# Transposing DMAs of the softmax weights beside the attention of a hybrid decoder trunk

## The chip, the core and the metric

The kernel runs on one core of a Trainium2 chip. The metric is the device time of one execution in microseconds. A core has TensorE (matmuls, in the profile PE, with its weight loads as PEld), VectorE (DVE), ScalarE (ACT), GpSimd (POOL) and SyncE (SP). SyncE computes nothing here; it issues nearly all DMAs, in the order of its queue, and a DMA that has to wait for something holds back every DMA behind it. A "q" behind an engine's name in the profile (SPq) means its sequencer.

## The reference

Two residual layers over one sequence of 1,024 positions and width 1,024, then a final RMS norm. The first layer is a gated linear recurrence (RG-LRU), the second forgetting attention with 16 heads of width 64, which is where the change lies:

```python
def one_block(args):
    q_blk, cq_blk, start = args
    qpos = start + jnp.arange(Q_BLOCK, dtype=jnp.int32)
    logits = jnp.einsum("bqhd,bkhd->bhqk", q_blk.astype(jnp.float32), kf) * scale
    logits = logits + (cq_blk[..., :, None] - ck[:, :, None, :])
    mask = kpos[None, :] <= qpos[:, None]
    logits = jnp.where(mask[None, None], logits, NEG_INF)
    p = jax.nn.softmax(logits, axis=-1)
    return jnp.einsum("bhqk,bkhd->bqhd", p, vf)
...
o = lax.map(one_block, (qb, cqb, starts))
...
y = o * jax.nn.silu(gate)
return y @ w_out.astype(h.dtype)
```

Queries go in blocks of 128 (`Q_BLOCK`). Block i, from 0 to 7, sees keys 0 to 128(i+1) - 1. `p`, the softmax weights of a block, is what the change touches.

## The kernel before, in words

All matmuls are done in split float32: each operand is divided into a high part (rounded to fp32r) and a low remainder, and three products are summed (`to_hi`, L85 and L87, mostly on ScalarE; `to_lo`, L96, on VectorE or GpSimd).

The first layer fills about the first 450 us. Attention follows, head by head. The work of a head is written as Python generators:

- `kq_units` and `g_units` project keys, queries and gates of the next pair of heads (products `gps`). `weights` loads each of their weight tiles `wf` (SyncE, L109) into one of three buffers and splits it into `wh` and `wl`. `values`, once in four heads, projects the values of the next two pairs (`vps`); in that stretch nothing else of a head runs.
- `load` and `load_q` (L604 to L618) copy a head's keys into tile T and its queries into tiles U, through SyncE. The tiles hold one head (T, two in turn) or half a head (U), so a copy waits until the matmuls of the head before have read the tile. The U of the first four blocks is one tile that all heads share.
- `maxima(hd, c)` takes blocks 4c to 4c + 3 of head hd. For each block it makes the logits S by matmuls of U and T (L54), adds the mask and finds the row maximum on VectorE (L715), and takes the exponential on ScalarE (L720), which writes `p` with its row sums. The tile of block i has one buffer for all heads, so block i of the next head overwrites it, about 29 us later. The exponential's instruction is kept in `seen`.
- `weigh(hd, c)` transposes p on TensorE by the identity (`pt`, L58), splits the result into `ph` and `pl` (three buffers each) and multiplies by the values (`O`). `scale` and `gated` multiply by the gate; `yo` is stored to DRAM by SyncE (L808).
- At the end `turned(c, q)` adds the output projection to the residual, transposed into rows (`turn`), takes squares for the norm (`sq1`, L931, ScalarE, in a tile `xp` with two buffers) and multiplies by the norm's weight.

`run` sets the order on TensorE: a hand-written string such as `1.0.1.1.1.0.0` says in which order the next step of `weigh` (0), of `maxima` for the coming half head (1) and of the filling projections (a dot) are taken. The order of the instructions on each engine, the DMAs in SyncE's queue among them, is fixed when the program is built; a planner may place instructions that no string orders, such as DMAs, by its own estimate.

Of the kernel before, what the change touches and what calls it, by code (L numbers as in the profile page):

```python
# [11 lines left out]
F32 = mybir.dt.float32  # L12
# [5 lines left out]
P = 128  # L18
SEQ = 1024
HALF = 512  # L20
# [18 lines left out]
def trunk(ctx: ExitStack, tc: tile.TileContext, xt, w0, wg, wo0, pc, gn, gf, w1, wv, wf, bf, wo1, out):  # L39
    nc = tc.nc  # L40

    def pool(name, bufs, **kw):
        return tc.tile_pool(name=name, bufs=bufs, **kw)
# [9 lines left out]
    def matmul(*args, **kw):  # L53
        pe[0] = nc.tensor.matmul(*args, **kw)  # L54
        return pe[0]
# [127 lines left out]
    with ExitStack() as l0:  # L183
# [9 lines left out]
        def long(tag, dtype=F32, bufs=1):  # L193
            return tmp.tile([P, SEQ], dtype, tag=tag, name=tag, bufs=bufs)
# [56 lines left out]
        sq = [z[:, cs] for z in (long("th"), long("ti")) for cs in halves]  # L251
# [240 lines left out]
    with ExitStack() as l1:  # L492
        tu = l1.enter_context(pool("tu", 1))
        at = l1.enter_context(pool("at", 2))
# [197 lines left out]
        def maxima(hd, c):  # L692

            s = hd % 2
            pair = hd // 2
            if c == 0:
                stats[hd] = at.tile([P, 8], F32, tag="sums", name="sums")
            sums = stats[hd]
            for i in range(4 * c, 4 * c + 4):
                n = (i + 1) * P  # L700

                o_ = 192 if i == 4 else 0
                S = ps.tile([P, SEQ], F32, tag="S", name="S")[:, o_:]
                u = U[s][c]
                qs = slice(i % 4 * P, i % 4 * P + P)
                for lo_, hi_ in ((0, min(n, HALF - o_)), (HALF - o_, n)):
                    if hi_ <= lo_:
                        continue
                    hi_ = max(hi_, lo_ + 256)
                    matmul(S[:, lo_:hi_], u[:, 0, qs], T[s][:, 0, lo_:hi_], start=True, stop=False)  # L710
                    matmul(
                        S[:, lo_:hi_], u[:96, 1, qs], T[s][:96, 1, lo_:hi_], start=False, stop=True
                    )
                m = at.tile([P, 1], F32, tag="m", name="m", bufs=4)
                nc.vector.tensor_tensor_reduce(  # L715
                    S[:, :n], S[:, :n], mask[:, SEQ - n :], -1.0, -NEG, ALU.add, ALU.min, accum_out=m
                )

                p = ps_[i] = at.tile([P, n], F32, tag=f"p{i}", name="p", bufs=1)
                seen[0] = nc.scalar.activation(  # L720
                    p, S[:, :n], AF.Exp, bias=m, scale=-1.0, accum_out=sums[:, i : i + 1]
                )
                yield
            if hd == HEADS - 1 or c == 1:
                b0, b1 = (4 * c if hd == HEADS - 1 else 0), 4 * c + 4
                nb = b1 - b0
                sums = sums[:, b0:b1]
                nc.vector.tensor_scalar(sums, sums, 2.0, None, ALU.mult)
                nc.vector.reciprocal(sums, sums)
                tr = ps.tile([P, P], F32, tag="O", name="tr")  # L730
                nc.tensor.transpose(tr[:nb], sums, ident)
                rc = at.tile([8, P], F32, tag="rc", name="rc", bufs=1)
                nc.vector.tensor_copy(rc[:nb], tr[:nb])
                nc.gpsimd.dma_start(recd[hd, b0:b1], rc[:nb])
                if s == 0:
                    recs[pair] = at.tile([P, SEQ], F32, tag="recb", name="recb", bufs=1)
                rows = slice(s * HD, (s + 1) * HD)
                nc.gpsimd.dma_start(
                    recs[pair][rows, b0 * P : b1 * P],
                    recd[hd : hd + 1, b0:b1].rearrange("o b q -> o (b q)").to_broadcast([HD, nb * P]),  # L740
                )
                yield
# [142 lines left out]
        def residual(c, q):  # L885

            cs = slice(q * 256, (q + 1) * 256)
            if c == q == 0:
                xs = [vpool.tile([P, 256], F32, tag=f"v{d}", name="x1", bufs=2) for d in range(KT)]
                for d, x in enumerate(xs):  # L890
                    nc.sync.dma_start(x, x1d[c, :, d, cs])
                return xs
            xs = [wpool.tile([P, 2, 256], F32, tag=("wl", "wh")[q], name="x1") for d in range(4)]
            for d, x in enumerate(xs):
                nc.sync.dma_start(x, x1d[c, :, 2 * d : 2 * d + 2, cs])
            return [x[:, i] for x in xs for i in range(2)]

        def turned(c, q):


            xs = left.pop((c, q), None) or residual(c, q)

            if c == 0:
                res = tu.tile([P, 2, SEQ], F32, tag=f"T{q}", name="res")
                res = [res[:, b] for b in range(2)]
            elif q == 0:
                res = [tu.tile([P, SEQ], F32, tag=t, name="res") for t in ("U", "U0")]
            else:
                res = [tu.tile([P, SEQ], F32, tag="U1", name="res"), at.tile([P, SEQ], F32, tag="p7", name="res", bufs=1)]
            for b in range(2):  # L910
                cs = slice(q * 256 + b * P, q * 256 + (b + 1) * P)

                parts = ((0, 4), (4, 2), (6, 2)) if c * q * b else ((0, 4), (4, 4))
                ss = ssq[c][:, 4 * q + 2 * b :][:, : len(parts)]
                for h, (d0, nd) in enumerate(parts):
                    hs = slice(d0 * P, (d0 + nd) * P)
                    pt = ps.tile([P, HALF], F32, tag="gO"[c * b] if h < 2 else "g", name="turn")[:, : nd * P]

                    for i in range(nd):
                        x = xs[d0 + i][:, b * P : (b + 1) * P]  # L920
                        matmul(pt[:, i * P : (i + 1) * P], x, ident, start=i == 0, stop=False, is_transpose=True)
                    for k in range(2):
                        yh, yl = (z[:, cs] for z in y1[c][6 + k])
                        wh, wl = (z[:, k::2][:, d0 % 4 : d0 % 4 + nd] for z in late_w[d0 // 4])
                        matmul(pt, yh, wh, start=False, stop=False)
                        matmul(pt, yl, wh, start=False, stop=False)
                        matmul(pt, yh, wl, start=False, stop=k == 1)
                        if k == 0:
                            yield
                    sq = at.tile([P, HALF], F32, tag="xp", name="sq1", bufs=2)[:, : nd * P]  # L930
                    nc.scalar.activation(sq, pt, AF.Square, accum_out=ss[:, min(h, ss.shape[1] - 1)].unsqueeze(1))  # L931
                    if c == 0 or h < len(parts) - 1:
                        nc.vector.tensor_tensor(res[b][:, hs], pt, grow[:, hs], ALU.mult)
                        if h == 1 and c == 1:
                            nc.vector.tensor_tensor(ss[:, 0:1], ss[:, 0:1], ss[:, 1:2], ALU.add)
                            ss = ss[:, 0::2]
                        yield
                if c == 1:
                    r = root_mean(ss, lambda: nc.vector.tensor_tensor(res[b][:, hs], pt, grow[:, hs], ALU.mult))
                    lo, hi = halves  # L940
                    nc.scalar.activation(res[b][:, lo], res[b][:, lo], AF.Copy, scale=r)
                    nc.vector.tensor_scalar(res[b][:, hi], res[b][:, hi], r, None, ALU.mult)
                    for hs in halves:
                        nc.sync.dma_start(out[4 + 2 * q + b, :, hs], res[b][:, hs])
                    yield
            if c == 0:
                first_half.extend(res)

        def root_mean(ss, between=lambda: None):

            ss = ss.rearrange("p (b h) -> p b h", h=2)
            r = ss[:, :, 0]
            nc.vector.tensor_tensor(r, r, ss[:, :, 1], ALU.add)
            between()
            nc.scalar.activation(r, r, AF.Sqrt, bias=epst, scale=1.0 / SEQ)
            nc.vector.reciprocal(r, r)
            return r
# [28 lines left out]
        load(0, halves[1], (1,))  # L986
        load(1, halves[1], (1,))
        run("00.0.0", maxima(0, 0), fill=fill)
        load_q(1, 0)
        drain(fill)  # L990
        for hd in range(HEADS):
# [31 lines left out]
            if hd % 4 == 3 and hd < 12:  # L1023

                vals = values(hd // 4 + 1)
                next(vals)
            run(second, weigh(hd, 1), maxima(hd + 1, 0), fill=fill, side=side)
            drain(side)
            gated(hd, 1)
# [93 lines left out]
```

## Time and profile before

| | |
|---|---|
| three runs | 1123.03, 1123.92, 1126.91 us; median 1123.92 |
| span of the profiled execution, the only time the page gives for it | 1127.7 us |
| instructions in the trace | 15,774 |
| TensorE, VectorE, ScalarE, GpSimd busy | 99%, 67%, 52%, 17% |
| DMA bytes | 105.43 MB, mean 93 GB/s |

The page gives, for each engine, the time in which it was busy, and then the chain that ended last: the work that, followed back from the last instruction, set the end. Issuing a DMA is not counted as busy time, so SyncE's load does not show among the busy shares; its queue shows in the list of DMA issues, in its waits and in the timeline. The views by windows give busy time in chosen stretches of the span, the views by tile or line the instructions that belong to it and what ended their waits.

### The profile page before, as it was taken

The numbers are of one execution on the slowest core, as the hardware profiler recorded it, in microseconds if no ns is written. First come the engines' busy times: TensorE is split into PE (matmuls) and PEld (weight loads), VectorE is DVE, ScalarE is ACT, GpSimd is POOL, SyncE is SP. The second block draws the span as 40 slices with busy tenths as digits, with TensorE's granted clock in tenths as the row PEclk, the third lists the DMA queues.
The fourth block names the chain that finished last, engine by engine and source line by source line (L and its number), as shares of the span: only waits on it lengthen the run. The fifth ranks groups of instructions, "written<-read, shape, count | busy, mean of one in ns | idle before, by whom it ended". The sixth has DMA issues, their size and how long they took to land.

```text
span 1127.7 us, 15774 instructions
## 1 busy us (share of the span) xinstructions
PE 1114.3 (99%) x5691; PEld 936.8 (83%) x5691; DVE 758.6 (67%) x1268; ACT 589.3 (52%) x1081; POOL 195.6 (17%) x155
## 2 busy tenths in 40 slices
PE   9999999999999999999999999999999999999997
PEld 7788888888888887988888988889888898888786
DVE  7888755776568789656676466664667646676545
ACT  8488345355453656365555355553555535644335
POOL 1322112221121201431021110212102110021220
PEclk9999999999999999999999999999999999999999
DMA  6111111111111114433425224242252422564345
GB/s 235 57 47 42 51 52 52 38 58 45 52 38 52 47 44 145 129 112 102 112 71 123 66 77 117 72 118 71 74 119 73 118 71 77 176 189 158 117 154 187
DMA packets 62902, 105.43 MB, mean 93 GB/s; under 512 B 9796, under 2 KB 24772, under 8 KB 62824
## 3 DMA queue, kind: packets, MB, share of 16 engines
q1 hardware_dynamic: 59704, 95.97, 28.9%
q0 software_dynamic: 3120, 8.46, 2.3%
q8 instruction: 45, 0.74, 0.3%
q14 instruction: 33, 0.27, 0.1%
HBM read 63.30 MB, written 15.93 MB: 70 GB/s over the span
## 4 chain that ended last, share of the span: by engine, by line
PE 92%; DMA 2%; DVE 2%; issue 1%; ACT 1%; SPq 1%; POOL 0%; DVEq 0%; POOLq 0%; ACTq 0%
PE gps L54 33%; PE ops L54 16%; PE ups L54 12%; PE vps L54 8%; PE S L54 6%; PE O L54 6%; PE pt L58 5%; PE gate L54 3%; PE turn L54 3%; DMA wf<-in_wo 1%; DMA x<-in_xt 1%; POOL wl L96 0%; PE rsrow L54 0%; DMA wf<-in_w 0%; DMA yhl<-y1d 0%
## 5 line engine op out<-in xcount | busy, mean ns | idle before, releaser
L54 PE MATMUL gps<-hh,wh 128*128 128x512 f32 x576 | 229.1, 398 | 0.6 <-DVE qkl L595 0.6
L54 PE MATMUL gps<-hh,wl 128*128 128x512 f32 x576 | 226.8, 394 | 0.0
L54 PE MATMUL gps<-hl,wh 128*128 128x512 f32 x576 | 226.7, 394 | 0.0
L85 ACT CAST wh<-wf 128x512 fp32r<-128x512 f32 (+2 forms) x156 | 94.2, 607 | 147.8 <-PE ops L54 55.3
L96 POOL TENSOR_TENSOR wl<-wf,wh 128x512 fp32r<-128x512 f32 (+1 forms) x60 | 101.0, 1689 | 389.8 <-ACT wh L85 362.5
L720 ACT ACTIVATE p<-S,m 128x128 f32<-128x128 f32 (+7 forms) x128 | 94.8, 741 | 137.9 <-DVE m L715 136.8
L96 DVE TENSOR_TENSOR pl<-pt,ph 128x512 fp32r<-128x512 f32 (+1 forms) x198 | 98.7, 540 | 88.1 <-ACT ph L85 87.6
L54 PEld LDWEIGHTS gps<-hl,wh 128*128 128x128 f32 x576 | 108.3, 188 | 24.7 <-issue 0.5
L54 PEld LDWEIGHTS gps<-hh,wh 128*128 128x128 f32 x576 | 108.6, 189 | 20.5 <-DVE qkl L595 0.8
L54 PEld LDWEIGHTS gps<-hh,wl 128*128 128x128 f32 x576 | 108.7, 189 | 20.1 <-POOL wl L96 0.6
L715 DVE CUSTOM_DVE_ANT_0 S<-S,mask 128x128 f32<-128x128 f32 (+7 forms) x128 | 97.3, 761 | 28.8 <-PE S L54 28.8
L85 ACT CAST ph<-pt 128x512 fp32r<-128x512 f32 (+1 forms) x198 | 83.6, 473 | 36.2 <-PE pt L58 28.9
L54 PE MATMUL S<-T,U 96*128 96x512 f32 (+7 forms) x384 | 91.9, 348 | 2.7 <-ACT p L720 2.7
L96 DVE TENSOR_TENSOR wl<-wf,wh 128x512 fp32r<-128x512 f32 x96 | 70.7, 741 | 28.3 <-ACT wh L85 27.4
L381 DVE TENSOR_TENSOR x<-x,ops 128x512 f32<-128x512 f32 x80 | 54.1, 683 | 48.0 <-PE ops L54 48.0
L54 PEld LDWEIGHTS S<-T,U 128*128 128x128 f32 (+1 forms) x384 | 68.6, 190 | 16.1 <-ACT p L720 3.5
L58 PE MATMUL pt<-ident,p 128*128 128x128 f32 x576 | 79.4, 273 | 0.8 <-DVE pl L96 0.5
L58 PEld LDWEIGHTS pt<-ident,p 128*128 128x128 f32 x576 | 67.2, 140 | 13.9 <-issue 2.9
L54 PE MATMUL ups<-hh,wh 128*128 128x512 f32 x192 | 76.1, 397 | 1.1 <-ACT hh L87 1.1
L54 PE MATMUL ups<-hl,wh 128*128 128x512 f32 x192 | 76.7, 399 | 0.2
L54 PE MATMUL ops<-yh,wh 128*128 128x512 f32 x192 | 76.0, 396 | 0.5 <-DVE x L474 0.5
L54 PE MATMUL ups<-hh,wl 128*128 128x512 f32 x192 | 76.2, 397 | 0.0
(183 smaller groups left out, 2247.8 us busy)
## 6 DMA issues: line engine op xcount, KB each, us to landing
wf<-in_w SPq DMA_DIRECT2D x100, 256.0 KB
wf<-in_wo SPq DMA_DIRECT2D x64, 128.0 KB
U<-qkh SPq DMA_DIRECT2D x64, 128.0 KB
T<-qkh SPq DMA_DIRECT2D x28, 256.0 KB
x<-in_xt SPq DMA_DIRECT2D x16, 256.0 KB
x1d<-x SPq DMA_DIRECT2D x16, 256.0 KB
wf<-in_wv SPq DMA_DIRECT2D x16, 256.0 KB
U<-qkl SPq DMA_DIRECT2D x32, 128.0 KB
```

The costliest lines, as they stand in the source:

```text
L54: pe[0] = nc.tensor.matmul(*args, **kw)
L58: pe[0] = nc.tensor.transpose(*args)
L85: nc.scalar.copy(hi, src)
L96: return eng.tensor_tensor(lo, src, f32(hi), ALU.subtract)
L381: nc.vector.tensor_tensor(x, x, pt, ALU.add)
L715: nc.vector.tensor_tensor_reduce(S[:, :n], S[:, :n], mask[:, SEQ - n :], -1.0, -NEG, ALU.add, ALU.min, accum_out=m)
L720: seen[0] = nc.scalar.activation(p, S[:, :n], AF.Exp, bias=m, scale=-1.0, accum_out=sums[:, i : i + 1])
```

## The change

In `maxima`, for heads 2 to 9, each block's `p` is read right behind its exponential by a DMA that transposes it: the float32 tile is taken as twice as many two-byte elements, and the result goes into `turned`, a tile of 128 partitions with 16 groups of 128 two-byte elements. That tile has one buffer, and nothing reads it. The DMA is issued from SyncE. The tile needs 4 KB per partition; to make room, the squares of the closing stage move from the two buffers of `xp` into those of `pl`, of which there are three. The output is the same.

```diff
@@ maxima @@
                 seen[0] = nc.scalar.activation(
                     p, S[:, :n], AF.Exp, bias=m, scale=-1.0, accum_out=sums[:, i : i + 1]
                 )
+                if 1 < hd < 10:
+                    turn = at.tile([P, 16, P], mybir.dt.uint16, tag="turned", name="turned", bufs=1)
+                    nc.sync.dma_start_transpose(turn[:, : 2 * i + 2], p.bitcast(mybir.dt.uint16))
                 yield
@@ turned @@
-                    sq = at.tile([P, HALF], F32, tag="xp", name="sq1", bufs=2)[:, : nd * P]
+                    sq = at.tile([P, HALF], F32, tag="pl", name="sq1", bufs=3)[:, : nd * P]
                     nc.scalar.activation(sq, pt, AF.Square, accum_out=ss[:, min(h, ss.shape[1] - 1)].unsqueeze(1))
```

## The prediction

> **What bounds the kernel now.** I read the page's busy table, its slices and its chain first, to see whether one engine sets the time.
>
> ```profile
> span 1127.7 us, 15774 instructions
> PE 1114.3 (99%) x5691; PEld 936.8 (83%) x5691; DVE 758.6 (67%) x1268; ACT 589.3 (52%) x1081; POOL 195.6 (17%) x155
> ...
> PE 92%; DMA 2%; DVE 2%; issue 1%; ACT 1%; SPq 1%; POOL 0%; DVEq 0%; POOLq 0%; ACTq 0%
> ```
>
> TensorE is busy for 99% of the span and makes 92% of the chain. Everything else is free as long as it hands TensorE its operands in time. The change adds nothing to TensorE, so it can cost only by being late. The profiled span of 1127.7 us is 3.8 us above the median of the runs, 1123.9; I work out a loss inside the profiled execution and add it to the median.
>
> The next view is busy time by stage, cut where the changed heads change pace. The cuts are the first exponential of head 2 (556.4), block 3 of head 4 (629.7), its block 4 (656.1), blocks 3 and 4 of head 8 (770.9 and 797.2), and the first of head 10 (839.4). Columns: length, then PE, PEld, DVE, ACT and POOL busy, clock, DMA share, GB/s.
>
> ```profile
> 556.40:629.70 73.30, 72.84 (x393) 61.83 (x392) 50.33 (x100) 37.88 (x86) 14.70 (x12) 1.00 0.39 101
> 629.70:656.10 26.40, 26.39 (x208) 25.48 (x208) 11.29 (x27) 11.13 (x28) 1.30 (x1) 1.00 0.22 67
> 656.10:770.90 114.80, 114.80 (x616) 97.68 (x615) 76.90 (x161) 60.78 (x139) 18.66 (x15) 1.00 0.36 97
> 770.90:797.20 26.30, 26.29 (x208) 25.38 (x207) 11.30 (x27) 11.11 (x27) 1.30 (x1) 1.00 0.19 62
> 797.20:839.40 42.20, 42.20 (x226) 35.78 (x226) 28.38 (x61) 22.97 (x52) 3.88 (x4) 1.00 0.34 87
> ```
>
> TensorE has no gap to give in any of the five; the clock is full. The second and fourth are the value projections, in which no exponential runs:
>
> ```profile
> 556.41 0.37 ACT L720 ACTIVATE p<-S,m 128x128 f32<-128x128 f32 x1
> 629.73 0.69 ACT L720 ACTIVATE p<-S,m 128x512 f32<-128x512 f32 x1 [1.89 <-DVE m L715]
> 656.08 0.79 ACT L720 ACTIVATE p<-S,m 128x640 f32<-128x640 f32 x1
> 770.90 0.69 ACT L720 ACTIVATE p<-S,m 128x512 f32<-128x512 f32 x1 [1.89 <-DVE m L715]
> 797.21 0.79 ACT L720 ACTIVATE p<-S,m 128x640 f32<-128x640 f32 x1
> 839.43 0.37 ACT L720 ACTIVATE p<-S,m 128x128 f32<-128x128 f32 x1
> ```
>
> **The change, part by part.** On TensorE, VectorE, ScalarE and GpSimd the built programs hold the same instructions in the same order. SyncE's queue gains 64 transposing DMAs, eight per head. Among the copies around them 43 change places, by at most five; the latest-moved are weight loads. Each transposing DMA waits for its block's exponential, and for the previous one to have landed, because the scratch tile has one buffer. All copies behind it in SyncE's queue wait too. So the stretches have to be seen as SyncE's schedule.
>
> *What must be moved.* Block i holds 128 rows of (i+1)*128 floats, taken as 2i+2 column groups of 128 two-byte elements. The built DMAs work in tiles of 16 rows by 128 columns (4,096 bytes, sixteen 256-byte rows). That is 16(i+1) tiles: 576 per head, 2.36 MB, 18.9 MB in all.
>
> *Fixed cost.* No transposing DMA is in the trace. The nearest rows are copies, issue to landing, and what SyncE takes to issue one:
>
> ```profile
> x1d<-xp POOLq DMA_DIRECT2D x16, 256.0 KB, 3.4
> recd<-rc POOLq DMA_DIRECT2D x15, 4.0 KB, 2.5
> L615 SPq DMA_DIRECT2D U<-qkh x32: 461/467/1236, 467.6 to 1008.2; - x32
> ```
>
> A copy with almost no bytes lands after 2.5 us; the 256 KB one's 3.4 is that and its bytes. Since each transpose waits for the last one's landing, a run of them takes 2.5 us apiece plus the moving of its tiles. A head's sixteen copies at 0.47 us (7.5 us) fit into the eight landings (20 us), so they add nothing.
>
> *Cost of a tile*, the unknown. The row to price it from is the hardware queue's:
>
> ```profile
> q1 hardware_dynamic: 59704, 95.97, 28.9%
> ```
>
> 28.9% of 16 engines for 1127.7 us is 5,215 engine-us for 95.97 MB. By bytes that is 294 GB/s over 16 engines, or 14 ns for a tile (lower end). By packets it is 87 ns each; a tile has sixteen rows, one per engine, so 87 ns if a short row costs what the mean packet of 1.6 KB does (upper end). A tile is read in rows and written turned, to 128 partitions; I charge its bytes once for each, 28 ns. This is nearer the row that counts bytes, because 256-byte rows should not cost what eight times as much does. A value below nothing is excluded: no work is removed.
>
> *What covers it.* A late SyncE queue costs nothing until a load comes too late. The tightest regular one I found is U for the next head's first block:
>
> ```profile
> 711.93 0.43 SPq L618 DMA_DIRECT2D U<-cumd  x1
> 726.84 0.46 PE L54 MATMUL S<-T,U 128*128 128x256 f32 x2
> ```
>
> Issued at 711.9 and landed 2.5 us later, it is first read at 726.8: 12.4 us of cover. T and the other U follow an earlier release and have more. When the cover is gone TensorE waits for each microsecond that SyncE is late. Next in line would be the exponential itself, which may not overwrite its block before the DMA has read it, about one head (29 us) later.
>
> *The sum*, stretch by stretch. A value projection lets SyncE catch up, so lateness starts again after each. With c in ns per tile:
> - Head 2 to block 3 of head 4: 20 DMAs, 1,312 tiles. 50 + 1.312c against 73.3 + 12.4 = 85.7.
> - Block 4 of head 4 to block 3 of head 8: 32 DMAs, 2,304 tiles. 80 + 2.304c against 114.8 + 12.4 = 127.2.
> - The rest, to the end of head 9: 12 DMAs, 992 tiles. 30 + 0.992c against 42.2 + 12.4 = 54.6.
>
> At c = 28: 86.7, 144.5 and 57.8, so losses of 1.0, 17.3 and 3.2, together 21.5 us. At c = 14 all three lie under their cover and the loss is nothing. Break-even is c = 20.5, in the middle stretch. At 87 the losses are 78.4, 153.2 and 61.7, together 293 us.
>
> The Trainium skill has a rule that would come out otherwise. "DMA: Bandwidth & Descriptors", section "Latency and other measured facts", gives a transposing DMA 261 GB/s: an estimate from it is 15.7 ns a tile, under the break-even, and no change. The same page, in the table of sequencer cycles under "Why a DMA increments its semaphore by 16 and not by 1", gives earlier generations 262,144 cycles for 8,192 tiles from SBUF to SBUF, 32 a tile. At the SyncE clock of 1.2 GHz in "Trainium Kernel Development and Optimization", section "NeuronCore Architecture", that is estimated at 26.7 ns, and the sum would be 16 us. No row here shows which of the two holds a transpose back.
>
> *The Square's scratch*, moved from two buffers of its own to the three of pl, frees room for the new tile. Its rows, in the closing stage:
>
> ```profile
> L931 ACT ACTIVATE sq<-turn x17: 372/597/602, 1090.4 to 1121.5; 128x512 f32<-128x512 f32 x15, 128x256 f32<-128x256 f32 x2
> ...
>   PE turn L54: 6.8, 9
> ...
>   DVE res L933: 6.1, 8
> ```
>
> The Square waits for TensorE's product, never for its buffer, and the last pl is used as this stage begins: nothing either way, between a gain of 6.1 us (all that VectorE waits for it) and a loss of one Square, 0.6.
>
> **Rivals.**
> - *Hidden.* A tile takes less than 22 ns and lateness stays under the cover: 1124 us. For it: the mean rate by bytes (14 ns) and a DMA share of only 0.34 to 0.39 in the changed stretches. Against it: 256-byte rows, and a single buffer that puts a full landing between any two. It gets a sixth of the chance, since the lower end lies well under the break-even. The Trainium skill's 261 GB/s, above, would make it so.
> - *Bound by small pieces.* The turned side goes out as 32-byte pieces (16 elements), and a tile takes over 50 ns. At 50 the losses are 29.9, 68.0 and 25.0: 123 us, 1247; at 87, 1417. For it: the packet price. Against it: only that price.
> - *Faster.* The Square's third buffer frees the closing stage, where VectorE waits 6.1 us for it: 1118. It decides only if the Square waits for a buffer and the transposes are hidden. Against it: the row above names TensorE alone.
>
> **How the numbers follow.** The forecast (22 to 50 ns, SyncE's queue late in the runs of heads without a value projection) has 0.63; its time at 28 ns is 1123.9 + 21.5, about 1146, and its own range 1127 to 1247. Hidden has 0.17, small pieces 0.16, faster 0.04. A difference under 0.3% (3.4 us) can't be told from none, and that is where hidden ends. Slower is 0.63 + 0.16 = 0.79, same 0.17, faster 0.04. The range reaches from 1121, below hidden, to 1247; it leaves out most of faster and what lies beyond 50 ns, 0.19.
>
> **What would show it.** Right: SyncE's waits for the exponentials and for the previous turned tile head its list; U's load before the first block of heads 5 to 8 comes 12 us or more late; TensorE waits before S<-T,U in the third stretch most, and the value stretches keep their 26 us; the other engines' busy time stays. Wrong: the exponentials of head 10 start 283 us after those of head 2, as now (hidden), or every head of the eight is longer by the same amount, the value stretches too (small pieces); or the stall first shows at another load, or at the exponential's own wait for its block, and the cover of 12.4 us was the wrong one.

## The result and the profile after

The changed kernel takes 1129.17 us, the median of 13 runs (1126.01 to 1141.67), against 1124.58 for 13 runs of the kernel before (1123.03 to 1128.69) on the same chip. The ratio is 1.0056, with a 95% interval of 1.0030 to 1.0082: slower by 0.6%, about 6 us by the ratio (the two medians differ by 4.6), where 21.5 were forecast.

The page of the kernel after: span and instructions, busy time by engine, the hardware queue's row (packets, MB, share of 16 engines), the chain by engine, and the group of the logits' matmuls (busy, mean ns, idle time before them and who ended it).

```profile
span 1126.9 us, 15939 instructions
PE 1113.8 (99%) x5691; PEld 935.8 (83%) x5691; DVE 758.2 (67%) x1268; ACT 589.4 (52%) x1081; POOL 194.5 (17%) x155
...
q1 hardware_dynamic: 135480, 114.85, 40.1%
...
PE 94%; DVE 2%; ACT 1%; DMA 1%; issue 1%; SPq 0%; DVEq 0%; ACTq 0%
...
L54 PE MATMUL S<-T,U 96*128 96x512 f32 (+7 forms) x384 | 92.2, 349 | 2.4 <-DMA U<-qkl 2.4
```

The engines' work is unchanged. What is new is 18.88 MB on q1 and a wait of 2.4 us for a load of U. The span looks shorter than that of before, 1127.7. That is the luck of one execution, as the waits of TensorE in the kernel before show (engine, its line, who released it, line: total us, times, longest):

```profile
PE S L54 <- ACT p L720: 2.7, 1, 2.7
```

In the execution profiled of the kernel before, TensorE once waited 2.7 us for an exponential, at 1049.9, far behind the changed heads. It lost that and something more, which the next view shows (length; PE, PEld, DVE, ACT, POOL busy; granted clock; DMA share; GB/s), in the kernel before:

```profile
1051.20:1054.60 3.40, 3.40 (x9) 2.67 (x8) 2.43 (x7) 0.78 (x2) 0.60 (x1) 0.50 0.15 51
```

The kernel before has such a dip in some executions and not in others, and three of the runs below in which it is absent have spans of 1121.7 to 1122.4. Against these, the 1126.9 of after is a loss of some 5 us.

The same view for the kernel after, in the five stretches of the prediction and then around the wait for U:

```profile
556.40:629.70 73.30, 73.30 (x396) 62.44 (x395) 50.39 (x100) 38.35 (x87) 14.15 (x11) 1.00 0.74 151
629.70:656.10 26.40, 26.39 (x207) 25.44 (x206) 11.98 (x28) 11.22 (x28) 1.29 (x1) 1.00 0.56 133
656.10:770.90 114.80, 111.84 (x586) 94.56 (x585) 75.31 (x156) 58.74 (x133) 18.21 (x15) 0.99 0.79 155
770.90:797.20 26.30, 26.30 (x205) 25.43 (x204) 9.81 (x24) 9.29 (x23) 1.29 (x1) 1.00 0.59 139
797.20:839.40 42.20, 42.19 (x226) 35.55 (x225) 28.78 (x59) 23.48 (x53) 3.49 (x3) 1.00 0.65 144
750.00:758.70 8.70, 6.64 (x33) 5.30 (x32) 5.14 (x12) 4.32 (x9) 0.57 (x1) 1.00 0.73 142
758.70:762.10 3.40, 3.10 (x12) 2.94 (x13) 1.05 (x3) 1.21 (x4) 0.54 (x1) 0.50 1.34 160
762.10:770.00 7.90, 7.90 (x44) 6.73 (x43) 4.90 (x10) 3.45 (x9) 3.52 (x2) 1.00 0.92 199
```

TensorE loses time in the middle stretch alone, where it is busy for 111.84 of 114.80, although the DMA share has about doubled or more in all five. Within that stretch it loses nearly all of this in one place: it idles before 759.0, and from 758.7 on the clock is at 0.50 for 3.4 us, in 3.10 of which TensorE is busy. Half clock for 3.10 us is 1.55 us of work not done, so this place costs 2.35 + 1.55 = 3.9 us. The exponentials agree. Head 10 starts 283.0 us after head 2 in the kernel before (556.41 to 839.43, in the prediction's rows); after, the timeline has:

```profile
555.91 0.37 ACT L720 ACTIVATE p<-S,m 128x128 f32<-128x128 f32 x1
...
843.32 0.37 ACT L720 ACTIVATE p<-S,m 128x128 f32<-128x128 f32 x1
```

That is 287.4 us, 4.4 more. The place itself, in the timeline of after (start, length, engine, line, operation, and in brackets the wait before it):

```profile
752.97 0.58 SPq L615 DMA_DIRECT2D U<-qkh  x1
753.60 0.59 SPq L616 DMA_DIRECT2D U<-qkh  x1
754.78 1.32 SPq L725 DMA_TRANSPOSE turned<-p  x1
756.20 0.63 SPq L617 DMA_DIRECT2D U<-qkl  x1
...
756.29 0.35 PE L54 MATMUL S<-T,U 128*128 128x256 f32 x1
759.00 0.55 PE L54 MATMUL S<-T,U 96*128 96x256 f32 x1 [2.35 <-DMA U<-qkl]
...
760.91 0.77 PE L54 MATMUL gps<-hh,wh 128*128 128x512 f32 x1
762.23 0.40 PE L54 MATMUL gps<-hh,wh 128*128 128x512 f32 x1
```

Head 8's first block needs four copies into U. A transposing DMA of head 7 stands between the third and the fourth in SyncE's queue. The load of the queries' low part is issued at 756.20. TensorE is through with the product before the one that reads it at 756.64 (756.29 + 0.35), and waits 2.35 us. The projection's matmul after it takes 0.77 us where the same one at full clock takes 0.40.

### The profile page after: what moved, and what is told of

It reads as the page before. It is cut to its first block, busy times and chain, and to the rows that moved or that the text cites. A ratio compares the mean times of both kernels' runs of the same rounds, so it can differ in the third digit from the quotient of the medians.

```text
span 1126.9 us, 15939 instructions
## 1 busy us (share of the span) xinstructions
PE 1113.8 (99%) x5691; PEld 935.8 (83%) x5691; DVE 758.2 (67%) x1268; ACT 589.4 (52%) x1081; POOL 194.5 (17%) x155
## 3 DMA queue, kind: packets, MB, share of 16 engines
q1 hardware_dynamic: 135480, 114.85, 40.1%
## 4 chain that ended last, share of the span: by engine, by line
PE 94%; DVE 2%; ACT 1%; DMA 1%; issue 1%; SPq 0%; DVEq 0%; ACTq 0%
PE gps L54 33%; PE ops L54 17%; PE ups L54 12%; PE vps L54 8%; PE O L54 6%; PE S L54 6%; PE pt L58 6%; PE gate L54 3%; PE turn L54 3%; DMA x<-in_xt 0%; PE rsrow L54 0%; DVE hl L247 0%; PE sscol L54 0%; ACT wh L85 0%; DMA wf<-in_w 0%
## 5 line engine op out<-in xcount | busy, mean ns | idle before, releaser
L85 ACT CAST wh<-wf 128x512 fp32r<-128x512 f32 (+2 forms) x156 | 94.3, 607 | 146.9 <-PE ops L54 55.5
```

Of the source, the lines that this page charges most:

```text
L85: nc.scalar.copy(hi, src)
```

## The experiments

The theory: each transposing DMA is slow and waits for the one before, SyncE's queue falls behind, and one load of U comes too late. The rivals: the 18.9 MB slow the other transfers, the Square's other scratch costs something, or there is nothing but the spread from run to run.

**The two kernels again.** `before_again` is the kernel before without any edit, `after_again` the changed kernel without any edit.

> The kernel before, unchanged. Theory L (late loads): each time TensorE waits more than about 2 us for a late U, the granted clock then halves for 3.4 us (the trace of after has it once, at 759), so the spread of clock 0.991 to 0.999 among the runs of the changed kernel comes from its late loads; here the clock lies at 0.997 to 0.999 in every run and the time within 1123 to 1129 us, ratio 1.000. Theory T (traffic): the transposes' bytes cost by themselves, through the clock or the DMA queues; the clock here lies higher than in the changed kernel too, so this run alone does not part them. Theory N (chance): clock and spread here are those of the changed kernel, 0.991 to 0.999.

> The changed kernel, unchanged. All theories: ratio 1.003 to 1.008. Theory L: the runs with a lower clock are the longer ones, about 2 us for each 0.001, and the profile has one wait or more for U of over 2 us in heads 4 to 9, each with a half-clock stretch of 3.4 us behind it. Theory T: the time is longer without such waits too, or the half-clock stretches stand where TensorE did not wait.

The unedited kernel gave 1.0001 (0.9987 to 1.0014) against itself, 1123.74 us in 12 runs, so 0.3% can be told from nothing. The changed kernel gave 1.0058 (1.0039 to 1.0078), 1130.76 us in 6 runs. Its longest waits on TensorE and the half-clock stretch in this second execution, the latter from the windows:

```profile
PE S L54 <- DMA U<-qkl: 2.4, 1, 2.4
PE S L54 <- DMA U<-qkh: 1.7, 1, 1.7
```

```profile
759.20:766.00 6.80, 5.36 (x18) 4.81 (x19) 2.41 (x6) 1.53 (x4) 1.08 (x2) 0.50 1.06 159
```

The place is the same, the start of head 8; this time two copies were late and the clock stayed at half for 6.8 us, two times 3.4, with TensorE busy for 5.36 of them. So the loss recurs at one spot, but its size varies: here 4.05 us of waits and half of 5.36, 2.7, for the clock, 6.7 together, against the 3.9 of the first execution. The mean loss of about 6 us lies between. Five of the first 13 runs took 1134 to 1142 us, at a mean granted clock of 0.991 to 0.996; none of these was profiled, so what they lose is not shown.

**Two of the 64 transposes fewer.** `skip_two` leaves out the scratch write of block 7 in heads 6 and 7, two of the longest; nothing reads what they would write.

```diff
-                if 1 < hd < 10:
+                if 1 < hd < 10 and not (i == 7 and hd in (6, 7)):
```

> Leaves out the transposing DMA of block 7 in heads 6 and 7 (2 of 64, 256 of 4,608 tiles, which nothing reads); the rest as in the changed kernel. In the trace of after each of these two takes SyncE about 4.5 us, and SyncE is 13 us late at the start of head 8. Theory L: the lateness at head 8 falls to some 4 to 5 us, under the cover of U; no wait for U over 1 us, no half-clock stretch between 556 and 850, ratio 0.999 to 1.002. Theory T: 94% of the bytes remain, so does the loss: ratio 1.004 to 1.006.

1127.43 us (12 runs, 1122.72 to 1133.32), ratio 1.0018 (1.0000 to 1.0037). The copy of U's low part at head 8 is issued at 752.52, 3.7 us earlier than after, and no wait for U is left in its profile (one of 2.5 us for an exponential stands near 1050, where the kernel before has one too). Of the two only head 6's stands ahead of that load (in the changed kernel they are issued at 735.59 and 769.26). One DMA, 128 of 4,608 tiles, was enough to take away some two thirds of the loss by the ratios (by their intervals, between a third and all of it), though 62 transposes remain; a cost spread evenly would have given back a thirtieth by the number of DMAs, an eighteenth by tiles.

**The late load on another queue.** `u_on_pool` keeps all 64 transposes and issues only the first U copies of heads 4, 6, 8 and 10 from GpSimd.

```diff
+            eng = nc.gpsimd if c == 0 and hd in (4, 6, 8, 10) else nc.sync
-            nc.sync.dma_start(f32(u[:64, 0]), hi)
+            eng.dma_start(f32(u[:64, 0]), hi)
...
```

> All 64 transposing DMAs as in the changed kernel, but the four copies of U for the first half of heads 4, 6, 8 and 10 are issued from GpSimd, not behind them in SyncE's queue. Theory L: TensorE's wait for U at head 8 goes, ratio 0.999 to 1.002, though SyncE stays as late (up to 15 us behind the exponentials). Theory T: all bytes are still moved, ratio 1.004 to 1.006.

1125.82 us (12 runs, 1123.32 to 1130.66), ratio 1.0017 (1.0003 to 1.0031). Three rows of its timeline: the load that was late, now on GpSimd, head 8's first exponential, and the transposing DMA that reads it.

```profile
746.25 0.52 POOL L618 DMA_DIRECT2D U<-qkl  x1 [0.34 <-DVE qkl L595]
...
757.86 0.37 ACT L721 ACTIVATE p<-S,m 128x128 f32<-128x128 f32 x1
...
777.04 1.17 SPq L726 DMA_TRANSPOSE turned<-p  x1
```

SyncE is 18.8 us behind the exponential here (757.86 + 0.37 to 777.04), later than in the changed kernel (13.4), and TensorE waits for no U. So what cost most was the load caught behind the queue, not the queue's lateness. All 18.9 MB and all transposes are still there; what they and the lateness cost by themselves is at most 0.3%, the upper end of the interval.

**Both together.** `both_fixes` has both edits.

> The two remedies together: 62 transposing DMAs (block 7 of heads 6 and 7 left out) and the four copies of U for the first half of heads 4, 6, 8 and 10 issued from GpSimd. Each alone left 1.0018 and 1.0017, at the edge of what can be told. Theory L with late loads alone: 0.999 to 1.001. Rival: a remainder of about 2 us that no load explains stays, 1.001 to 1.003.

1124.81 us in 12 runs against 1123.68 in 23, ratio 1.0005 (0.9992 to 1.0018): no difference that these runs could tell. The 0.17 to 0.18% that either leaves alone is at the edge of what these runs tell; whether a smaller cost remained there is not settled by them.

The traces show where it is not. From head 2's first exponential to head 10's, the profiled executions without transposes took 283.0 us (before), 284.0 (before_again) and 282.4 (square_only), those of skip_two, u_on_pool and both_fixes 283.6 to 283.7, and those of two_groups and plain_copy (below) 283.0 and 283.7, against 287.4 and 289.8 in the two of the changed kernel. So with the late load gone, no more than about 1 us is left in the changed heads. The wait for an exponential near 1050, far behind them, came in before (2.7 us), before_again (2.1), skip_two (2.5) and both_fixes (3.1, with a stretch of half clock), and as none over 1 us in after, after_again, u_on_pool, square_only, plain_copy and two_groups; whether the transposes make it more frequent is not shown.

**The other parts of the change, each alone.** `square_only` makes no transpose and moves only the Square's scratch. `plain_copy` writes the same bytes into the same tile by a DMA that doesn't turn them. `two_groups` turns only the first two column groups of each block, 1,024 tiles in place of 4,608, and leaves the rest of the scratch unwritten.

```diff
# plain_copy
-                    nc.sync.dma_start_transpose(turn[:, : 2 * i + 2], p.bitcast(mybir.dt.uint16))
+                    nc.sync.dma_start(turn[:, : 2 * i + 2].rearrange("p a b -> p (a b)"), p.bitcast(mybir.dt.uint16))
# two_groups
+                    nc.sync.dma_start_transpose(turn[:, :2], p[:, :P].bitcast(mybir.dt.uint16))
```

> No transposing DMA at all; only the square's scratch moves from its own two buffers to the three of pl. Theory L and the prediction: nothing, ratio 0.999 to 1.001. Rival: the move is part of the 0.56%, ratio 1.001 to 1.003.

> Each transposing DMA is a plain copy of the same bytes into the same tile at the same place in SyncE's queue, with the same waits; nothing is turned. Theory L: what makes SyncE late is the time of a tile (20 to 25 ns in the trace of after) and the landing. 4 KB of plain copy take 14 ns at the queue's mean rate and SyncE is held only for the 0.5 us of an issue, so in the middle stretch some 32 x 2.2 + 2,304 x 0.014 = 103 us of queue stand against 114.8: no lateness at head 8, ratio 0.999 to 1.002. Rival (any DMA of these bytes, turned or not): ratio 1.004 to 1.007.

> All 64 transposing DMAs, but each turns only the first two column groups of its block (16 tiles; 1,024 tiles in all instead of 4,608). If the fixed cost of a DMA (wait for the last landing, 2.5 us in the prediction) were what makes SyncE late, lateness would stay at about half; by the prices of after (1.4 to 1.9 us fixed, 27 ns a tile) SyncE is less than 3 us late at head 8 and the ratio 0.999 to 1.001.

| | median us (runs) | ratio (95%) | SyncE's largest lateness |
|---|---|---|---|
| square_only | 1124.01 (10) | 0.9994 (0.9975 to 1.0013) | - |
| plain_copy | 1124.04 (10) | 0.9994 (0.9974 to 1.0013) | 5.8 us |
| two_groups | 1124.27 (10) | 1.0006 (0.9995 to 1.0016) | 3.2 us |

The Square's move costs nothing that these runs could tell, to within 0.2%. The same holds of the 18.87 MB copied without turning, and of 64 transposing DMAs of two groups each. It takes the turning of whole blocks to make SyncE more than 11 us late. Two rows of plain_copy, the queue's and the DMA's own (instructions: least, median and largest ns of hold on SyncE, first and last start), and the latter of after:

```profile
q1 hardware_dynamic: 68920, 114.85, 34.5%
...
L725 SPq DMA_DIRECT2D turned<-p x64: 464/478/1291, 557.8 to 842.1; - x64
```

```profile
L725 SPq DMA_TRANSPOSE turned<-p x64: 1168/1340/3763, 557.3 to 846.9; - x64
```

A transposing DMA holds SyncE's sequencer 1.34 us (median), a copy of the same bytes 0.48.

**Twice the transposes.** `twice` turns each block two times.

```diff
-                    nc.sync.dma_start_transpose(turn[:, : 2 * i + 2], p.bitcast(mybir.dt.uint16))
+                    for _ in range(2):
+                        nc.sync.dma_start_transpose(turn[:, : 2 * i + 2], p.bitcast(mybir.dt.uint16))
```

> Each block is turned twice, one transposing DMA right behind the other into the same tile. With the prices measured in after (per DMA about 2.3 us with the copies between, 1.55 us for a second one right behind it, 23.5 ns a tile) and a cover of 8.8 us, theory L gives 77 + 61.7 - 82.1, 123.2 + 108.3 - 123.6 and 46.2 + 46.6 - 51.0 us of lateness in the three stretches, 206 us together, some 20 more for half-clock stretches: 1320 to 1360 us. Theory T (cost by bytes): twice 6 us, 1137.

1285.79 us (2 runs), ratio 1.1421 (1.1373 to 1.1469): less than expected. TensorE's longest waits, from its list of waits, ScalarE's wait for the transposing DMAs, from its own list, and the busy row of the page:

```profile
PE pt L58 <- ACT p L720: 35.2, 9, 5.9
PE S L54 <- ACT p L720: 30.4, 10, 5.0
PE S L54 <- DVE pl L96: 22.8, 4, 12.5
PE O L54 <- ACT ph L85: 12.3, 3, 7.0
PE S L54 <- DMA U<-qkh: 6.9, 1, 6.9
...
ACT p L720 <- DMA turned<-p: 103.2, 28, 8.7
```

```profile
PE 1159.7 (90%) x5691; PEld 963.9 (75%) x5691; DVE 756.8 (59%) x1268; ACT 590.3 (46%) x1081; POOL 194.9 (15%) x155
```

Now SyncE is up to 56 us behind, more than the 29 us for which a block's tile is free, and the wait that the prediction put next in line comes: the exponential may not overwrite a block that the DMA has not read (28 waits of ScalarE, 103.2 us), and TensorE waits for it. TensorE's five waits add to 108 us. TensorE's busy time grows by 46 us (1159.7 against 1113.8) with the same matmuls: the mean granted clock is 0.947. The loss is steep once the cover is gone: the first 64 transposes cost 6 us and the next 64 a further 155.

**The transposes on ScalarE's queue.** `queue_act` issues them from ScalarE, right behind the exponential.

```diff
-                    nc.sync.dma_start_transpose(turn[:, : 2 * i + 2], p.bitcast(mybir.dt.uint16))
+                    nc.scalar.dma_start_transpose(turn[:, : 2 * i + 2], p.bitcast(mybir.dt.uint16))
```

> The 64 transposing DMAs are issued from ScalarE instead of SyncE. Theory L: U is no longer late, but each holds ScalarE for 1.2 to 2 us and until the last one has landed, some 11 to 20 us a head beside 15 us of work, in 29: the casts come late and TensorE waits for ph; 1140 to 1200 us. Rival (which queue does not matter, the bytes do): 1130.

1226.95 us (2 runs), ratio 1.0899 (1.0856 to 1.0941), more than expected. Two rows of its page: the transposes have a queue of their own there, and TensorE waits for ScalarE.

```profile
q10 hardware_dynamic: 75776, 18.88, 9.3%
...
L54 PE MATMUL S<-T,U 96*128 96x512 f32 (+7 forms) x384 | 95.5, 357 | 23.2 <-ACT p L720 23.0
```

Freeing SyncE doesn't help if ScalarE pays: each DMA holds ScalarE's sequencer as long as it held SyncE's (median 1.33 us), and the sequencer's wait in front of it, up to 5.7 us, delays all that ScalarE has to do next, the exponentials among it. The row of q10 also prices the turning alone: 9.3% of 1225.5 us is 114.0 us of all sixteen engines for 4,608 tiles, 24.7 ns a tile.

A version with two scratch tiles, which would take away the wait between two transposes, would need 4 KB more per partition; it wasn't tried.

## Why the prediction was wrong in size

Direction, place and range held (the range by 2 us at its lower end): slower, by a late SyncE queue, in the middle stretch, at U of head 8; the value projections kept their 26 us and lateness started again after each (exponential to transpose 10.2 us at block 3 of head 4 and 0.1 at block 4; 11.1 and 0.1 at head 8). The step that failed is the sum of the middle stretch: 144.5 us of queue, 17.3 over its cover, so that a load would come 29.7 us late against a cover of 12.4. The load of U at head 8 came 10.7 us late against a cover of some 8.7. The terms mis-sized are the fixed cost (2.5 us where 1.7 was measured), the copies (nothing where 22 us were measured) and the cover. The other two stretches, 1.0 and 3.2 forecast, lost nothing. By its steps:

- **What must be moved:** right; 18.88 MB and 4,608 tiles came.
- **Cost of a tile, 28 ns:** nearly right. q1 took 40.1% of 1126.9 us after and 28.9% of 1127.7 before, 126.0 us more of all sixteen engines, 27.3 ns a tile. The share of q1 without transposes varies (30.0% of 1122.1 us in square_only), which puts it between 25 and 28, and q10 gives 24.7. In the packets' records a tile is sixteen packets of 256 bytes, 24 ns each, where the prediction's packet price was 87. The plain copy, by the same two subtractions, took 11 to 13.3 ns for the same 4,096 bytes: the lower end, 14, was a fair price for bytes alone. The 261 GB/s of the Trainium skill ("DMA: Bandwidth & Descriptors", section "Latency and other measured facts") isn't reached: 4,096 bytes in 25 to 28 ns are 146 to 164 GB/s.
- **Fixed cost, 2.5 us: too high, and the largest error on that side.** It was borrowed from the landing of a tiny copy. Two pairs of transposes in the timeline of after, the first of each with 64 and 112 tiles, the second waiting for its landing:

```profile
605.62 1.24 SPq L725 DMA_TRANSPOSE turned<-p  x1
608.74 1.32 SPq L725 DMA_TRANSPOSE turned<-p  x1
...
809.91 1.53 SPq L725 DMA_TRANSPOSE turned<-p  x1
813.92 1.74 SPq L725 DMA_TRANSPOSE turned<-p  x1
```

  3.12 us for 64 tiles and 4.01 for 112: 48 tiles more take 0.89 us, 18.5 ns each, and the rest, 1.9 us, doesn't depend on the size. In the packets' records of q1 the same time is 1.18 us from issue to the first packet, and at least 0.52 from the last packet to the next issue, 1.7 together; the packets themselves take 20.5 ns a tile undisturbed and 24.7 on average, other transfers beside them. With 1.7 and 24.7 the middle stretch is 32 × 1.7 + 2,304 × 0.0247 = 111 us, under its 114.8.
- **"Copies fit into the landings, so they add nothing": wrong the other way.** The queue was 11 to 13 us late at the end of that stretch (head 8's first exponential ended at 760.35, its transposing DMA was issued at 773.73). From the issue of the stretch's first transposing DMA (655.95) to that of its last (786.56) are 130.6 us. In the packets' records 31 times 1.7 are 52.7 of it and the moving of 2,240 tiles is 55.5; the remaining 22 are, but for less than 1 us, what the copies between and the waits in front of them took.
- **Cover, 12.4 us: not the tightest.** Three rows of the kernel before, and the same load after:

```profile
604.33 0.46 SPq L617 DMA_DIRECT2D U<-qkl  x1
745.49 0.46 SPq L617 DMA_DIRECT2D U<-qkl  x1
...
756.48 0.46 PE L54 MATMUL S<-T,U 128*128 128x256 f32 x2
```

```profile
610.17 0.65 SPq L617 DMA_DIRECT2D U<-qkl  x1
690.46 0.64 SPq L617 DMA_DIRECT2D U<-qkl  x1
756.20 0.63 SPq L617 DMA_DIRECT2D U<-qkl  x1
```

  For even heads U follows the query projection closely; that the other U have more cover was wrong. At head 8 the low part was issued at 745.49, and the second of the two products of 756.48, which reads it, began at 756.65: 11.2 us. Its last packet ended 1.9 us after the issue, and TensorE went on some 0.55 us behind that packet in both executions of the changed kernel, so the cover is an estimated 8.7 us. The changed kernel issues the load 10.7 us later, 2.0 beyond the cover, its last packet comes 0.3 us later after the issue than before, and 2.35 was the wait. At head 4 it is 5.8 us later, within the cover, and TensorE doesn't wait. So with the right cover the "lateness minus cover" rule fits the place and the size of the wait.
- **What a wait costs: missed.** The forecast charged one microsecond per microsecond late. The stretch at half clock that comes with the wait, 3.4 us or twice that, adds 1.55 us (after) to 2.7 (after_again).
- **Square:** nothing, as forecast. **Hidden** lost by 2 us of lateness. **Small pieces** fell with 24 to 28 ns a tile. **What would show it:** SyncE's waits for the previous turned tile came (67.7 us in 48 waits), but as fourth of its list, and those for the exponentials were 6.7 us only; the late U of heads 5 to 8 and the waits in stretch after stretch did not, only head 8's.

In numbers, for the 31 steps of the 130.6 us: the forecast's prices give 31 × 2.5 + 2,240 × 0.028 = 140.2 us. The fixed cost in it is 24.8 us too high, the tiles are 7.2 too high, and the copies 22.4 too low. That the direction came out right is partly luck: with the right price of a DMA and of a tile, and still nothing for the copies, the same sum gives 111 us, under the stretch's 114.8, and no loss. The errors cancelled in part, and what was forecast is a small difference of large sums.

## What to carry to other kernels

The price of a DMA whose result nobody reads is set by what stands behind it in its queue: look for the load with the least time between its issue and its first reader, in every head and not in a typical one, and compare that time with how late the queue gets. A loss of the form "queue time minus cover" from sums of over 100 us can't be sized to a few microseconds by prices borrowed from other operations; give it as a threshold, with the load that would cross it. Moving the late load and its like in three other heads to another engine's queue took the wait away while all the extra transfers stayed; moving the slow DMAs to a busy engine's queue cost 9%.

## What the runs showed of the hardware

- A short wait of TensorE can be dearer than its length. With waits of 2.35 us (after), 2.69 (before, another place) and 3.12 (both_fixes) the granted clock is 0.50 for 3.4 us; in after_again, with 1.66 and 2.39, for 6.8. The half clock begins 0.3 us before the wait's end in after and both_fixes, 1.4 before it in after_again, and 1.3 behind it in before. With single waits of 2.06 (before_again) and 2.49 (skip_two) it stayed full, so the length alone doesn't decide. The Trainium skill, "TensorE: Matmul & The Clock Gate", section "Part 1: The HAM clock gate (the "warmup" mystery)", has a clock of two states, full and half, set by activity over free-running windows of 3413 ns. The 0.50 and the 3.4 us agree, and windows that run free of the kernel would let the same wait pass or not; that last point these runs don't prove. Its account that half clock follows an idle window of some 3.4 us fits less well: 2.35 us of waiting sufficed.
- A transposing DMA holds the sequencer that issues it for 1.2 us even with 16 tiles, 0.7 more than a plain copy (0.48). With 112 tiles it is 1.5 to 2.4, so most of it doesn't depend on the size. The runs don't show why.
- Turning costs DMA time as well: 24 to 28 ns for each 4,096 bytes, against 11 to 13.3 for a plain copy of the same bytes within the chip's on-chip memory.
